# Six numbers of the mixers' scheduling tables in a hybrid attention and convolution layer: four priority offsets, two filler counts

## Chip, cores and metric

The kernel runs on one core of one Trainium2 chip. The metric is the device time of one execution in microseconds (us), given as the median of several runs.

## What is computed

One layer of a hybrid trunk, on x of 1 x 2048 x 1024 in float32. The mixers are sliding-window attention (8 query heads of 64, 2 key/value heads, blocks of 128, window 128, a learned sink per head) beside a gated short convolution of width 512. An MLP of 1024 to 4096 to 1024 with squared relu follows. Cut to what matters:

```
h = rms_norm(x, attn_norm_g)
z = h @ w_in                       # q, k, v, gate_b, gate_c, xc
q, k = rms_norm(q, q_norm_g), rms_norm(k, k_norm_g)
y_attn = swa_sink_attention(q, k, v, sinks)
y_conv = gate_b * short_conv(gate_c * xc, conv_w)
y = concatenate([rms_norm(y_attn, attn_out_g), rms_norm(y_conv, conv_out_g)])
x = x + y @ w_out
hm = rms_norm(x, mlp_norm_g)
x = x + square(relu(hm @ w_up)) @ w_down
```

## The kernel before

**Tiles and stages.** Each float32 operand of a large product is split in a high and a low part, and a product takes three matmul passes, lines 278, 279 and 280 of the helper `mm3`. The sequence is worked in four chunks of 512 positions, stages 0 to 3 here, of four blocks of 128 each; the blocks are b0 to b15, so stage 1 holds b4 to b7 and stage 3 holds b12 to b15. After the mixers the MLP follows: seven products in place of eight for each level of its blocks, up in line 1454 and down in line 1571, about 64% of the span.

**Attention of a block.** `qk_transpose` puts q and k on the partitions (matmuls ptq_b and ptk_b of L697 and L699, the splits into high and low parts of qt_b and kw on ScalarE and VectorE in L702 to L707). `softmax` makes the scores (matmuls psc_b, L724), copies and masks them (L732, L735), reduces the maximum (L737, L738), takes eight exponentials (L741) and the denominators (L745 to L748), and scales the probabilities (L749). `values` turns the probabilities (ptp_b, L760), splits them (ScalarE L766, VectorE L767; GpSimd masks them, L773, into pp_b), splits v into vz and vd (L787, L788), multiplies (po_b, L812: two matmuls with vz, then two with vd, for each of the two key/value heads), and moves the result out (L820, L821) and into the split operand at_b of the output projection (L824, L825). L826 to L828 and the tiny matmul pa_b (L833), copied in L835, give the attention norm.

**Work beside it.** TensorE is kept going by steps that have nothing to do with the block at hand: the generator `besides` yields after every three matmuls. In a stage they are the attention half of the output projection of the chunk before (pout, moved out by VectorE in L963), the convolution's products (pc_c, px_c, pb_c), the convolution half of this chunk's output projection (pout of yt_c, L963 too), the norm and transposition of the next chunk (L294, pt_a L306, L310, L311) and its projection pz. In stage 3, where there is no next chunk, the attention half of its own projection runs at its end, and `x_blocks` prepares operands of the MLP: it loads rows (L362), scales them (L368), transposes them on TensorE (pt_m, L374), puts them back with a gain on VectorE (L375), stores blocks to memory over the queue of SyncE (SP; xop, L345), and makes differences of blocks in place on VectorE (L388), which are stored too. An L388 that overwrites a block has to wait until the store that reads it has landed. SP also issues the weight loads (L247).

**What sets the order.** Two tables. `FILL[c]` says how many of those steps are pulled at which place of stage c: FILL[c][0] before and after the first scores, and FILL[c][t+1] at five places for block t, the fourth of them in `values` just ahead of the first po_b matmuls and the fifth between the two heads. `PRIO[stage][i]` is an offset with which the instructions of one part are put ahead of (positive) or behind (negative) others by the scheduler that writes each engine's order: 0 qk_transpose, 1 softmax, 2 the q and k norm of the next block, 3 the attention norm, 4 the first part of values, 5 the po_b matmuls, 6 the moving out of values, 7 the weights' splits, 8 the norm of `prepare`, 9 its transposition, 10 the convolution, 11 the moving out of the projection (L963), 12 and 13 the two parts of `x_blocks`. The fifth row of PRIO is that of what follows the mixers. Once written, the order of each engine is fixed, and each engine takes its instructions strictly in it.

**PSUM.** Three banks hold the products pout, pc_c, px_c, pb_c, pz ("mm"), four the attention, one the transpositions (pt_a, pt_m). A product that needs a bank waits until what stood there has been moved out, so L963 gives back an "mm" bank and L375 gives back the transposition bank.

Of the kernel before, what the change touches and what calls it, by code (L numbers as in the profile page):

```python
# [84 lines left out]


PRIO = (
# [5 lines left out]
)  # L93

FILL = (
# [4 lines left out]
)  # L100


# [1508 lines left out]
```

## Time and profile before

| | |
|---|---|
| median of 3 runs | 1916.22 us (1916.06 to 1918.76) |
| profiled execution | 1920.32 us |
| its span | 1918.6 us |
| TensorE (PE) busy | 1910.4 us, 8930 matmuls |
| VectorE (DVE), ScalarE (ACT), GpSimd (POOL) busy | 1202.4, 829.4, 276.2 us |
| start of the first ptq_b of b0, b4, b8, b12, and of the first MLP matmul | 45.3, 187.0, 357.3, 524.0, 695.2 us |

A row of the timeline gives the start in us, the duration in us, engine, line, operation, out<-in by name without numbers, sizes, how many neighbours are taken together, and in brackets the idle time of the engine before it with what ended it. A matmul's shown duration is modelled and longer than the distance to the next one; distances between starts tell what a matmul costs. A row of the table by stretches of time gives the stretch, its length, then for PE, PEld (weight load), DVE, ACT and POOL the busy us and in brackets the instructions, then the granted TensorE clock, the busy share of the DMA engines and GB/s.

### The profile page before, as it was taken

Reading aid. Unit: us, or ns where it says so; the run is one execution under the profiler, and the core shown is the slowest. Engines: PE = TensorE matmul, PEld = TensorE weight load, DVE = VectorE, ACT = ScalarE, POOL = GpSimd, SP = SyncE. Lnnn points to the kernel's source line nnn. Section 1 sums busy time; section 2 is a strip of 40 time slices with the busy share of each in tenths; the row PEclk is TensorE's granted clock in tenths of the full one; section 3 lists DMA queues with packets and bytes.
Section 4 is the critical chain, followed back from the end, with each engine's and each line's share of the span. In section 5 each row is a group of like instructions: output and inputs, shape, how many; then the busy total and the mean of one; then the engine's idle time right before and its main releaser. Section 6 shows DMA issues by size and latency. Waiting matters only on the chain.

```text
span 1918.6 us, 24557 instructions
## 1 busy us (share of the span) xinstructions
PE 1910.4 (100%) x8930; PEld 1592.5 (83%) x8930; DVE 1202.4 (63%) x1857; ACT 829.4 (43%) x1557; POOL 276.2 (14%) x477
## 2 busy tenths in 40 slices
PE   9999999999999999999999999999999999999999
PEld 8888888888888888888888888888888888888887
DVE  4895567448467759999778766766534334457531
ACT  5564345335444446444555545554322332232320
POOL 2123212312221112233101111111000000100000
PEclk9999999999999999999999999999999999999999
DMA  8984854564577688768566444438954456866631
GB/s 280 337 325 125 328 198 176 205 234 154 201 273 259 215 301 242 229 215 247 192 224 224 164 161 146 150 138 320 367 200 148 138 175 221 284 223 213 218 126 55
DMA packets 232792, 413.80 MB, mean 216 GB/s; under 512 B 51672, under 2 KB 136416, under 8 KB 219872
## 3 DMA queue, kind: packets, MB, share of 16 engines
q1 hardware_dynamic: 203696, 336.33, 51.8%
q0 software_dynamic: 15424, 51.40, 6.9%
q10 hardware_dynamic: 13552, 24.52, 3.4%
q8 instruction: 70, 1.15, 0.2%
q14 instruction: 50, 0.41, 0.1%
HBM read 286.35 MB, written 125.83 MB: 215 GB/s over the span
## 4 chain that ended last, share of the span: by engine, by line
PE 96%; DMA 2%; DVE 1%; ACT 1%; SPq 0%; POOL 0%; issue 0%; ACTq 0%; DVEq 0%
PE u L1454 32%; PE d L1571 32%; PE pout L278 3%; PE pout L280 3%; PE pout L279 3%; PE pz L278 2%; PE pz L280 2%; PE pz L279 2%; PE psc_b L724 1%; PE px_c L280 1%; PE px_c L278 1%; PE px_c L279 1%; PE pb_c L280 1%; PE po_b L812 1%; PE pb_c L279 1%; PE pb_c L278 1%
## 5 line engine op out<-in xcount | busy, mean ns | idle before, releaser
L1454 PE MATMUL u<-op_x,wop 128*128 128x512 f32 x2688 | 610.2, 389 | 0.0
L1571 PE MATMUL d<-op_w,op_f 128*128 128x512 f32 x2691 | 609.5, 389 | 0.0
L1454 PEld LDWEIGHTS u<-op_x,wop 128*128 128x128 f32 x2688 | 504.4, 188 | 105.6 <-DVE wop L453 0.4
L1571 PEld LDWEIGHTS d<-op_w,op_f 128*128 128x128 f32 x2691 | 505.0, 188 | 104.5
L434 DVE TENSOR_TENSOR op_f<-op_f 128x1024 fp32r<-128x1024 f32 x112 | 137.0, 1225 | 237.2 <-ACT op_f L433 237.2
L433 ACT CAST op_f<-op_f 128x1024 fp32r<-128x1024 f32 x112 | 117.7, 1051 | 353.1 <-DMA op_f<-fop 342.5
L452 ACT CAST wop<-wu 128x512 fp32r<-128x512 f32 x156 | 96.3, 620 | 92.4 <-PE u L1454 89.3
L453 DVE TENSOR_TENSOR wop<-wu,wop 128x512 fp32r<-128x512 f32 x156 | 111.2, 714 | 33.6 <-ACT wop L452 18.5
L1190 POOL DMA_DIRECT2D fop<-s x96 | 52.1, 542 | 441.8 <-DVE s L1193 437.3
L1196 DVE TENSOR_TENSOR u<-u,u 128x512 f32<-128x512 f32 x128 | 88.0, 687 | 19.0 <-PE u L1454 18.7
L434 DVE TENSOR_TENSOR op_w<-raw,op_w 128x1024 fp32r<-128x1024 f32 x56 | 68.4, 1223 | 25.4 <-ACT op_w L433 25.2
L433 ACT CAST op_w<-raw 128x1024 fp32r<-128x1024 f32 x56 | 58.8, 1051 | 45.0 <-PE d L1571 22.6
L1202 ACT ACTIVATE u<-u 128x512 f32<-128x512 f32 x64 | 40.5, 632 | 53.8 <-DVE u L1196 51.5
L741 ACT ACTIVATE sc_b<-sc_b,ngm_b 128x128 f32<-128x128 f32 x128 | 49.7, 390 | 29.4 <-DVE ngm_b L738 29.4
L773 POOL TENSOR_SCALAR_AFFINE_SELECT pp_b<-pp_b 128x512 fp32r<-128x512 f32 x60 | 41.2, 700 | 133.9 <-ACT pp_b L766 66.0
L1403 POOL DMA_DIRECT2D wds<-raw x16 | 8.5, 533 | 330.0 <-DVE raw L1401 330.0
L453 DVE TENSOR_TENSOR wop<-wu_s,wop 128x512 fp32r<-128x512 f32 x64 | 46.0, 720 | 11.4 <-ACT wop L452 11.2
L452 ACT CAST wop<-wu_s 128x512 fp32r<-128x512 f32 x64 | 39.4, 620 | 30.0 <-PE u L1454 26.8
L278 PE MATMUL pout<-w_wo,yt_c 128*128 128x512 f32 x128 | 51.5, 402 | 0.0
L280 PE MATMUL pout<-w_wo,yt_c 128*128 128x512 f32 x128 | 51.0, 398 | 0.0
L724 PE MATMUL psc_b<-kw,qt_b 128*128 128x256 f32 (+1 forms) x256 | 49.3, 285 | 1.1 <-DVE qt_b L703 0.8
L279 PE MATMUL pout<-w_wo,yt_c 128*128 128x512 f32 x128 | 50.3, 393 | 0.0
(265 smaller groups left out, 3106.4 us busy)
## 6 DMA issues: line engine op xcount, KB each, us to landing
op_f<-fop SPq DMA_DIRECT2D x112, 512.0 KB, 4.4
raw<-in_w_down_dram SPq DMA_DIRECT2D x72, 512.0 KB, 4.1
wu<-in_w_up_dram SPq DMA_DIRECT2D x128, 256.0 KB, 3.7
w_wo<-wo SPq DMA_DIRECT2D x24, 1024.0 KB, 6.8
fop<-s POOLq DMA_DIRECT2D x96, 256.0 KB, 2.6
fop<-u ACTq DMA_DIRECT2D x64, 256.0 KB, 2.6
op_x<-xop SPq DMA_DIRECT2D x28, 512.0 KB, 6.4
w_q<-q SPq DMA_DIRECT2D x12, 1024.0 KB, 6.7
```

Source lines behind the costliest of these rows:

```text
L278: nc.tensor.matmul(ps, st(0), mv(0), start=first, stop=False)
L279: nc.tensor.matmul(ps, st(0), mv(1), start=False, stop=False)
L280: last_sum[0] = nc.tensor.matmul(ps, st(1), mv(0), start=False, stop=last).ins
L433: nc.scalar.copy(op[:, 0], raw)
L434: nc.vector.tensor_tensor(op[:, 1], raw, op[:, 0].bitcast(F32), op=ALU.subtract)
L452: splits.append(nc.scalar.copy(hi, blk).ins)
L453: lows.append(nc.vector.tensor_tensor(lo, blk, hi.bitcast(F32), op=ALU.subtract).ins)
L724: nc.tensor.matmul(ps[:, j].rearrange("p s k -> p (s k)")[:, :nk], qt[:, pr, j, :], kw[:, r, kv, :, :].rearrange("p s k -> p (s k)")[:, :n ...
L1190: eng.dma_start(fop_dram[tb][ORDER_DOWN.index(i)][n // 2][:, n % 2], b)
L1196: return nc.vector.tensor_tensor(dst, ps, b, op=ALU.add).ins
L1454: nc.tensor.matmul(pt, wops[i][:, a, k, :], xops[tb, p][k // 2][:, b, k % 2, :], start=p not in GOES_ON and k + j == 0, stop=k + j == NB + ...
L1571: nc.tensor.matmul(ps[tb][j][:, cs], fs[tb][:, a, k, j * P : (j + 1) * P], w[:, b, k, cs], start=first and p not in GOES_ON and k + n == 0 ...
```

## The change

Four entries of PRIO and two of FILL get other numbers. No instruction is added or removed on any engine.

```diff
-    (60, 0, 160, -10, 30, 0, 20, -10, -20, 30, 0, 300, 0, 0),
-    (220, -60, -60, -50, 40, 0, 20, 40, -60, 280, 0, 0, 0, 0),
+    (60, 0, 160, -10, 30, 0, 20, -10, -20, 30, 0, 320, 0, 0),
+    (220, -60, -60, -50, 40, 0, -10, 40, -60, 280, 0, 0, 0, 0),
...
-    (200, 20, 180, 240, 0, 0, 40, 40, 240, 0, 0, 30, 0, 0),
-    (160, 80, 0, 10, 0, 0, 20, -20, -20, 0, 0, 120, 0, 0),
+    (200, 20, 0, 240, 0, 0, 40, 40, 240, 0, 0, 30, 0, 0),
+    (160, 80, 0, 10, 0, -10, 20, -20, -20, 0, 0, 120, 0, 0),
...
-    ((25, 15), (9, 16, 11, 8, 1), (9, 8, 13, 3, 2), (13, 12, 15, 6, 5), (9, 14, 11, 5, 3)),
+    ((25, 15), (9, 16, 11, 9, 1), (9, 8, 13, 3, 2), (13, 12, 15, 6, 5), (9, 14, 11, 5, 3)),
...
-    ((27, 6), (9, 9, 5, 6, 3), (6, 7, 7, 5, 5), (8, 13, 8, 7, 8), (11, 3, 10, 1, 2)),
+    ((27, 6), (9, 9, 5, 6, 3), (6, 7, 7, 5, 5), (8, 13, 8, 7, 8), (11, 3, 10, 4, 2)),
```

Each number made by itself in the kernel before, with the rest left as it was, moves the following. PRIO[0][11] (300 to 320) and PRIO[4][5] (0 to -10) move no row of any engine. PRIO[1][6] (20 to -10) and FILL[1][1][3] (8 to 9) move rows of stage 1. PRIO[3][2] (180 to 0) moves rows of stage 3 from b12 to b14. FILL[3][4][3] (1 to 4) moves rows at the end of stage 3, at b15. The rows of stage 0 and of the MLP stand in the same order on every engine, and so do those of stage 2 but for one L684 on VectorE at its start, which falls behind one L963.

The first place is TensorE at the end of stage 3, where block b15 multiplies its probabilities (po_b) beside the first half of the last output projection (pout). Before:

```order
L280 MATMUL pout_0_0_0_6647<-w_wo_0_6505,at_b_5845 128x512
L812 MATMUL po_b_0_6651<-pp_b_0_0_6602,vz 128x512
L278 MATMUL pout_0_0_0_6647<-w_wo_0_6505,at_b_5845 128x512
L279 MATMUL pout_0_0_0_6647<-w_wo_1_6506,at_b_5845 128x512
L812 MATMUL po_b_0_6651<-pp_b_0_0_6602,vz 128x512
L812 MATMUL po_b_0_6651<-pp_b_0_1_6603,vd 128x512 x2
L280 MATMUL pout_0_0_0_6647<-w_wo_0_6505,at_b_5845 128x512
```

The same place with the change:

```order
L280 MATMUL pout_0_0_0_6647<-w_wo_0_6505,at_b_5845 128x512
L812 MATMUL po_b_0_6661<-pp_b_0_0_6602,vz 128x512 x2
L812 MATMUL po_b_0_6661<-pp_b_0_1_6603,vd 128x512 x2
L278 MATMUL pout_0_0_1_6666<-w_wo_0_6505,at_b_6156 128x512
L279 MATMUL pout_0_0_1_6666<-w_wo_1_6506,at_b_6156 128x512
```

Before, the four po_b matmuls of the first head began after three of the twelve matmuls of the first pout; now they stand together behind all twelve. Those of the second head stand behind six matmuls of the next pout, and pa_b of b15 stands after six matmuls of the fourth pout instead of after nine of the third. On VectorE the L963 of the first pout goes ahead of b15's two L821.

The second place is VectorE in stage 3, where the softmax of b12 and the scores of b13 (sc_b_5452 and sc_b_5603) run beside the blocks of `x_blocks` (xt_m); rows with - are of before, those with + of the change:

```order
 L375 TENSOR_TENSOR xt_m_0_5440<-pt_m_0_1_5583,g_cols 128x512
 L747 TENSOR_TENSOR den_b_5488<-den_b_5488,es_b_5497 128x8
-L388 TENSOR_TENSOR xt_m_0_5440<-xt_m_0_5440 128x512
+L735 COPY_PREDICATED sc_b_5603<-later,psc_b_0_5604 128x128
 L748 RECIPROCAL den_b_5488<-den_b_5488 128x8
 L735 COPY_PREDICATED sc_b_5603<-later,psc_b_0_5604 128x128
 L749 TENSOR_TENSOR sc_b_5452<-sc_b_5452,den_b_5488 128x1024
-L735 COPY_PREDICATED sc_b_5603<-later,psc_b_0_5604 128x128
 L735 COPY_PREDICATED sc_b_5603<-later,psc_b_1_5612 128x128 x2
+L388 TENSOR_TENSOR xt_m_0_5440<-xt_m_0_5440 128x512
 L735 COPY_PREDICATED sc_b_5603<-later,psc_b_2_5620 128x128 x2
```

The first L388 of these blocks stands now behind the scaling of b12 (L749) and three more L735. On TensorE the transpositions of the two blocks just ahead of this place stand four matmuls earlier (pt_m of xt_m_0_5439, second half) and two matmuls earlier (pt_m of xt_m_0_5440, first half), and the four psc_b_3 of b12 stand together instead of one by one between pc_c matmuls; on SP one xop store goes ahead of one load of x, two ahead of another, and later one ahead of a weight load.

The third place is VectorE in stage 1, where L963 moves out the convolution half of chunk 1's output projection (pout_1_0_0 and on, one for each block of 128) while b5 is moved out (o_b, at_b) and b6 is in its softmax (den_b, sc_b). Before, beginning with the L963 of the first pout:

```order
L963 SCALAR_TENSOR_TENSOR x_1_0_3041<-pout_1_0_0_3073,rc_2148,x_1_0_3041 128x512
L827 TENSOR_TENSOR o_b_3100<-o_b_3100 128x256
L963 SCALAR_TENSOR_TENSOR x_1_1_3043<-pout_1_0_1_3131,rc_2148,x_1_1_3043 128x512
L311 TENSOR_TENSOR h_h_3050<-pt_a_1_4_3246,h_h_3049 128x4x128
L828 TENSOR_TENSOR o_b_3100<-o_b_3100 128x128
L747 TENSOR_TENSOR den_b_2891<-den_b_2891,es_b_2900 128x8
L963 SCALAR_TENSOR_TENSOR x_1_2_3045<-pout_1_0_2_3148,rc_2148,x_1_2_3045 128x512
L748 RECIPROCAL den_b_2891<-den_b_2891 128x8
L735 COPY_PREDICATED sc_b_3187<-later,psc_b_0_3188 128x128
L749 TENSOR_TENSOR sc_b_2855<-sc_b_2855,den_b_2891 128x1024
```

With the change:

```order
L747 TENSOR_TENSOR den_b_2894<-den_b_2894,es_b_2903 128x8
L821 TENSOR_TENSOR o_b_3104<-po_b_1_3099,o_b_3104 64x512
L748 RECIPROCAL den_b_2894<-den_b_2894 128x8
L963 SCALAR_TENSOR_TENSOR x_1_0_3010<-pout_1_0_0_3073,rc_2148,x_1_0_3010 128x512
L749 TENSOR_TENSOR sc_b_2858<-sc_b_2858,den_b_2894 128x1024
L311 TENSOR_TENSOR h_h_3019<-pt_a_1_4_3246,h_h_3018 128x4x128
L825 TENSOR_TENSOR at_b_3109<-o_b_3104,at_b_3109 128x512
L963 SCALAR_TENSOR_TENSOR x_1_1_3012<-pout_1_0_1_3095,rc_2148,x_1_1_3012 128x512
L963 SCALAR_TENSOR_TENSOR x_1_2_3014<-pout_1_0_2_3148,rc_2148,x_1_2_3014 128x512
```

The softmax of b6 (L747, L748, L749) has moved from behind the L963 of the second and third pout to ahead of them, and the L821 of b5's second head stands ahead of the first. On TensorE po_b of b5 and ptq_b of b7 come three matmuls later, and on ScalarE the eight exponentials of b6 go ahead of the L820 of b5's second head.

## Prediction

> **What bounds the kernel now.** I read the page's head first, then the table by stretches of time, then the waits of TensorE (PE).
>
> ```profile
> span 1918.6 us, 24557 instructions
> PE 1910.4 (100%) x8930; PEld 1592.5 (83%) x8930; DVE 1202.4 (63%) x1857; ACT 829.4 (43%) x1557; POOL 276.2 (14%) x477
> ```
>
> ```profile
> 200.00:400.00 200.00, 200.00 (x1015) 169.03 (x1014) 114.06 (x240) 84.36 (x234) 47.49 (x80) 1.00 0.61 233
> 400.00:600.00 200.00, 198.71 (x1029) 166.64 (x1028) 127.14 (x257) 93.25 (x245) 40.49 (x72) 1.00 0.56 208
> 600.00:700.00 100.00, 99.64 (x486) 82.72 (x485) 65.09 (x125) 35.11 (x90) 18.26 (x39) 1.00 0.70 239
> 700.00:800.00 100.00, 100.00 (x443) 82.84 (x442) 89.01 (x130) 61.52 (x101) 21.14 (x39) 1.00 0.85 263
> 582.00:585.00 3.00, 3.00 (x19) 2.56 (x17) 2.89 (x6) 0.43 (x1) 1.03 (x3) 1.00 0.43 107
> 555.00:582.00 27.00, 26.92 (x146) 22.64 (x145) 19.91 (x46) 18.15 (x57) 2.40 (x6) 1.00 0.90 319
> ```
>
> ```profile
> PE idle L579 <- POOL ident L172: 1.6, 1, 1.6
> PE psc_b L724 <- DVE qt_b L703: 0.8, 1, 0.8
> PE po_b L812 <- POOL pp_b L773: 0.4, 1, 0.4
> PE psc_b L724 <- DVE kw L706: 0.3, 1, 0.3
> ```
>
> ```profile
> 1911.80 2.91 PE L1571 MATMUL d<-op_w,op_f 128*128 128x512 f32 x15
> ```
>
> TensorE is the bound: of 1918.6 us it is idle in 1918.6 - 1910.4 = 8.2. Of these 1.6 are its wait for the identity matrix at the start, and 1918.6 - 1914.7 = 3.9 lie behind the last matmuls (1911.80 + 2.91), so that under 3 us of waits are left in the whole program. From 200 to 400 us, where stage 1 lies, it is idle for 0.00 us; from 400 to 600 for 1.29; in the first 100 us of MLP for none, the three other engines being busy less. An order that only moves work can win what TensorE waits, and little else: its matmuls are the same 8930. That caps a gain at a fifth of a per cent before anything else is known, and losses have no such cap.
>
> The Trainium skill, page "Perfetto Trace Analysis", section "Identifying the Most-Contended Engine", says that matmul busy time is no measure of TensorE's headroom and that the busy share of the weight loads is to be used. Taken so, 83% would leave 17% of the span, some 326 us, to win, and the cap above would be wrong. The rows speak against it here: from 700 to 800 us TensorE has no gap, and its weight loads are busy for 82.84 of 100 us.
>
> The profiled execution took 1920.32 us, 4.1 above the median of 1916.22. The terms below are differences of start times within that one execution, and I put them on the median.
>
> **Term 1, FILL[3][4][3] from 1 to 4 (end of stage 3, b15).** A matmul of 512 columns is followed by the next one after 0.23 us; what a row stands later than that is loss.
>
> ```profile
> 672.27 0.40 PE L812 MATMUL po_b<-pp_b,vd 128*128 128x512 f32 x1
> 673.03 0.50 PE L812 MATMUL po_b<-pp_b,vd 128*128 128x512 f32 x1 [0.36 <-POOL pp_b L773]
> 673.37 0.40 PE L280 MATMUL pout<-w_wo,at_b 128*128 128x512 f32 x1
> 673.60 0.39 PE L278 MATMUL pout<-w_wo,at_b 128*128 128x512 f32 x1
> ...
> 681.55 0.40 PE L278 MATMUL pout<-w_wo,at_b 128*128 128x512 f32 x1
> ```
>
> ```profile
> 671.95 2.31 POOL L773 TENSOR_SCALAR_AFFINE_SELECT pp_b<-pp_b 128x512 fp32r<-128x512 f32 x3 [0.21 <-DVE pp_b L767]
> ```
>
> ```profile
> 677.40 0.68 DVE L825 TENSOR_TENSOR at_b<-o_b,at_b 128x512 fp32r<-128x512 f32 x1
> ```
>
> The second vd matmul of the first head starts 673.03 - 672.27 = 0.76 after the first, 0.53 too late, and the next one 0.34 after it, 0.11 too late: 0.64 us. It waits for GpSimd's second masking: three take 2.31 us from 671.95, about 0.77 each, so that the first of them is done at about 672.7 and the last at 674.3. In the new order nine more pout matmuls stand ahead of the first po_b, and its second vd starts at about 674.0, the second head's at about 676.1. Both are behind what they need, by 1.3 and 1.8 us, and the wait goes: **-0.64 us**. What is late next? The second head's results come 1.4 us later (676.35 in place of 674.96 for its last matmul), and so does the split L825, which ended at 677.40 + 0.68 = 678.08; counting that the second pout's L963 now goes ahead of it, it ends at about 679.7. The first matmul that reads it stood at 681.55 and will stand at about 680.8. That leaves 1.1 us, and pa_b, which went six matmuls further back, about 0.4. Bounds: -0.64 and 0, the latter if one of these margins is used up.
>
> **Term 2, PRIO[3][2] from 180 to 0, at the transpositions.**
>
> ```profile
> 563.00 0.39 PE L278 MATMUL pc_c<-h_h,w_wc 128*128 128x512 f32 x1
> 563.47 0.66 PE L374 MATMUL pt_m<-ident,xt_m 128*128 128x128 f32 x4
> ```
>
> ```profile
> 562.52 0.30 DVE L735 COPY_PREDICATED sc_b<-later,psc_b 128x128 f32<-128x128 int32 x1
> 562.73 0.68 DVE L375 TENSOR_TENSOR xt_m<-pt_m,g_cols 128x512 f32<-128x512 f32 x1
> 563.33 1.21 DVE L737 TENSOR_REDUCE ngm_b<-sc_b 128x8 f32<-128x1024 f32 x1
> 564.46 0.68 DVE L375 TENSOR_TENSOR xt_m<-pt_m,g_cols 128x512 f32<-128x512 f32 x1
> ```
>
> The transposition of 563.47 waits for the bank that L375 gives back at 563.41 and starts 0.24 late. Four matmuls earlier it would be due at about 562.5, before that L375 is through. But b12's last scores, which VectorE's queue needs ahead of it, also come together and up to 0.8 us earlier, so that the wait stays about as long. The transposition behind it then wants the bank at about 563.9, and its L375 is queued behind the reduction L737 of 1.21 us. It could cost 0.24 + 0.1 more, or the earlier scores could clear the way. Value **0**, bounds -0.3 (the late start goes) and +0.4.
>
> **Term 3, the same number, at the stores.** The longest wait of the mixers' later part hangs on a store.
>
> ```profile
> 593.63 0.39 PE L278 MATMUL pb_c<-h_h,w_wb 128*128 128x512 f32 x1
> 594.31 0.39 PE L724 MATMUL psc_b<-kw,qt_b 128*128 128x256 f32 x1 [0.28 <-DVE kw L706]
> ...
> 594.91 0.40 PE L280 MATMUL pb_c<-h_h,w_wb 128*128 128x512 f32 x1
> 596.07 0.50 PE L724 MATMUL psc_b<-kw,qt_b 128*128 128x256 f32 x2 [0.77 <-DVE qt_b L703]
> ```
>
> ```profile
> 591.91 0.69 DVE L388 TENSOR_TENSOR xt_m<-xt_m,xt_m 128x512 f32<-128x512 f32 x1 [2.23 <-DMA xop<-xt_m]
> ```
>
> ```profile
> 570.13 0.63 SPq L247 DMA_DIRECT2D w_wc<-wc  x1
> ...
> 582.93 0.32 SPq L247 DMA_DIRECT2D w_wx<-wx  x1
> 583.44 2.31 SPq L345 DMA_DIRECT2D xop<-xt_m  x2
> ```
>
> ```profile
> w_wx<-wx SPq DMA_DIRECT2D x1, 1024.0 KB, 7.8
> xop<-xt_m SPq DMA_DIRECT2D x1, 256.0 KB, 8.0
> ```
>
> Here TensorE loses 0.45 + 0.93 = 1.4 us. The chain back: scores of b14 need qt_b and kw from VectorE, VectorE stood still for 2.23 us at an L388, and that waits for the store issued at 583.44, which needed 8.0 us because the 1 MB load issued half a us ahead of it shares the engines. Between VectorE's L388 and those scores the change moves nothing. But earlier, the second place in the order rows, the first L388 stands behind an L749 and three L735, some 1.9 us later: L749 takes 1.22 (its row stands in term 4) and an L735 0.2 (562.52 to 562.73). Its store is issued later, and SP, which works in order, issues the 1 MB load w_wc of 570.13 later too. From 555 to 582 us the DMA engines are 0.90 busy, so a delay can be carried on; from 582 to 585, just ahead of the store in question, they are 0.43 busy, so it has room to end. I take the latter, the nearer row: **0**. Bounds: +1.9 if the whole delay arrives, and -1.4 if the shift by chance brings the store home before VectorE comes to it.
>
> **Term 4, FILL[1][1][3] from 8 to 9 and PRIO[1][6] from 20 to -10 (stage 1).** TensorE has no idle time there, so there is nothing to win beyond 0.1 us of late starts.
>
> ```profile
> 303.71 0.74 DVE L963 SCALAR_TENSOR_TENSOR x<-pout,rc,x 128x512 f32<-128x512 f32 x1
> ...
> 307.15 1.22 DVE L749 TENSOR_TENSOR sc_b<-sc_b,den_b 128x1024 f32<-128x1024 f32 x1
> ```
>
> The L963 give back the product banks, and the softmax rows L747, L748 and above all L749 with its 1.22 us now stand between the first two of them, with b5's L825 besides. Three banks and groups of twelve matmuls at 0.23 give a bank about 5.4 us until it is wanted again, and the queue is some 2.6 us longer ahead of the second L963: it should mostly fit, with little left for the fourth pout. Value **+0.2**, bounds -0.1 and +1.2 (one L749 in full).
>
> **PRIO[0][11] and PRIO[4][5]** move no row on any engine: 0.
>
> **Sum.** -0.64 + 0 + 0 + 0.2 = -0.44 us: 1916.22 - 0.44 = **1915.8 us**, and the profiled execution of 1920.32 by the same sum 1919.9. A difference of 0.2% here is 3.8 us, about what a measurement of this kernel can tell from no change; the forecast is no change.
>
> **The rivals.**
>
> *The store comes later (ends slower).* Term 3 takes its upper end: the delay of up to 1.9 us goes from L388 through the stores and the w_wc load to the store at 583.44, VectorE stands still that much longer, and TensorE waits for qt_b. 1916.22 - 0.64 + 1.9 = 1917.5. For it: 0.90 busy DMA and strict order on SP. Against it: the 0.43 just ahead. It decides the sign as soon as that store lands over 0.64 us later than before.
>
> *The stage 1 banks run out (slower).* Term 4 takes 1.2: 1916.22 - 0.64 + 1.2 = 1916.8. For it: the L749 between two L963. Against it: the 5.4 us and a stage without a gap.
>
> *It doesn't do what it says.* Two of the six numbers are dead, and the wait of term 1 may only move to the next reader (at_b or pa_b of b15): 1916.2.
>
> *The store's wait goes by chance (faster).* 1916.22 - 0.64 - 1.4 = 1914.2, or -0.11%.
>
> *TensorE falls back to a slow phase.* At the start it runs at half rate:
>
> ```profile
> 6.64 2.08 PE L555 MATMUL pz<-w_q,h_a 128*128 128x512 f32 x4 [0.45 <-ACT w_q L593]
> ...
> 11.88 2.31 PE L555 MATMUL pz<-w_q,h_a 128*128 128x512 f32 x9
> ```
>
> Four matmuls in 2.08 us, then nine in 2.31, 0.52 against 0.26 each, and the change comes some 8 us after the first matmul at 1.58. If a wait in stage 3 grew so long that this came back, it would cost the growth, about 2.6 us from 0.77, and half of some 8 us: 1916.22 - 0.64 + 2.6 + 4 = 1922.2. Against it: the longest gap is 0.77 us, and the granted clock is 1.00 in every stretch shown (it is given as 1.00 in the slow start too, so the row can't exclude a short phase). The Trainium skill, page "TensorE: Matmul & The Clock Gate", section "🔬 Part 1: The HAM clock gate (the "warmup" mystery)", puts the clock at half after an idle window of about 3.4 us and needs as much steady work to lift it; the start agrees in its factor of two, and no row in the middle of this run shows a fall.
>
> **How the numbers follow.** Forecast 0.50, with its own range of 1915.1 to 1916.4; the later store 0.18; banks 0.12; nothing done 0.08; the store's wait gone 0.07; slow phase 0.05. Faster by over 0.2% needs below 1912.4, that is all the waits named here and another 1.5 us: 0.02, out of the store's wait gone. Slower by over 0.2%, above 1920.1, is the slow phase: 0.05. Within: 0.93. The range goes from 1913.9, the store's wait gone and term 2's 0.3 with it, to 1918.7, where the later store and the banks come together (1916.22 - 0.64 + 1.9 + 1.2).
>
> **What would show it.** Term 1: the wait of po_b for GpSimd's pp_b is gone from TensorE's waits, and none for at_b or o_b has come. Term 2: the starts around pt_m at 562 to 564 us. Term 3: how long that store takes and whether VectorE's 2.23 us before L388 is longer or shorter; psc_b's waits of 0.8 and 0.3 follow it. Term 4: still 200.00 busy from 200 to 400 us. A change of over 2 us either way would make the prediction wrong in its reasons, since no wait but that of the store has so much to give.

## The result, and the profile after

The changed kernel takes **1921.09 us** (median of 12 runs, 1918.0 to 1923.92) against **1916.25 us** for the kernel before in the same comparison (12 runs, 1915.45 to 1920.28). The ratio is 1.0017, with a 95% interval of 1.0009 to 1.0025: slower by about 3 us. The ratio is not the quotient of the two medians, which lie 4.84 us apart; its interval reaches from 1.7 to 4.8 us. The forecast was 1915.8 and the range ended at 1918.7, so the measured time lies above it.

The profiled execution took 1923.0 us. The head of its page, and its table by stretches of time with the columns as before (PE busy, then PEld, DVE, ACT, POOL, the granted clock, the DMA share, GB/s):

```profile
span 1921.3 us, 24566 instructions
PE 1909.6 (99%) x8930; PEld 1590.3 (83%) x8930; DVE 1203.0 (63%) x1857; ACT 828.1 (43%) x1557; POOL 277.5 (14%) x477
```

```profile
200.00:400.00 200.00, 199.41 (x1010) 168.22 (x1009) 113.85 (x239) 83.91 (x234) 48.38 (x80) 1.00 0.61 231
400.00:600.00 200.00, 198.22 (x1026) 166.31 (x1025) 125.55 (x254) 92.46 (x244) 40.20 (x71) 1.00 0.58 211
```

The work is the same. TensorE is idle for 11.7 us of the span, it was 8.2, and stage 1, which had no gap, has 0.6. Its waits:

```profile
PE pz L555 <- ACT w_q L593: 1.6, 1, 1.6
...
PE ptq_b L697 <- ACT sc_b L732: 1.0, 1, 1.0
PE psc_b L724 <- DVE qt_b L703: 0.8, 1, 0.8
PE pa_b L833 <- DVE o_b L828: 0.8, 2, 0.6
PE psc_b L724 <- DVE kw L706: 0.6, 1, 0.6
PE u L1454 <- DVE wop L453: 0.4, 1, 0.4
PE pt_m L374 <- DVE xt_m L375: 0.4, 1, 0.4
PE u L1454 <- ACT wop L452: 0.3, 1, 0.3
PE u L1454 <- ACT u L1209: 0.2, 1, 0.2
```

The wait of po_b for GpSimd is gone. New are pa_b behind VectorE's L828, pt_m behind L375, and three waits of the MLP's u, which stands in the part of the program whose order didn't change. Term 1's place on TensorE:

```profile
674.66 0.61 PE L812 MATMUL po_b<-pp_b,vz 128*128 128x512 f32 x2
675.11 0.62 PE L812 MATMUL po_b<-pp_b,vd 128*128 128x512 f32 x2
675.56 0.39 PE L278 MATMUL pout<-w_wo,at_b 128*128 128x512 f32 x1
```

The two vd matmuls take 675.56 - 675.11 = 0.45 us together, the full rate. Terms 2 and 3, TensorE and then VectorE:

```profile
562.84 0.39 PE L280 MATMUL pc_c<-h_h,w_wc 128*128 128x512 f32 x1
563.61 0.66 PE L374 MATMUL pt_m<-ident,xt_m 128*128 128x128 f32 x4 [0.39 <-DVE xt_m L375]
```

```profile
562.87 0.68 DVE L375 TENSOR_TENSOR xt_m<-pt_m,g_cols 128x512 f32<-128x512 f32 x1
```

```profile
593.27 0.69 DVE L388 TENSOR_TENSOR xt_m<-xt_m,xt_m 128x512 f32<-128x512 f32 x1 [2.57 <-DMA xop<-xt_m]
```

The transposition is 563.61 - 562.84 - 0.23 = 0.54 us late, it was 0.24: it comes earlier in the order, the L375 that gives its bank back doesn't (562.87 + 0.68 = 563.55). VectorE stands still for 2.57 us ahead of L388, it was 2.23. And the MLP on TensorE near 995 us:

```profile
993.62 1.52 PE L1454 MATMUL u<-op_x,wop 128*128 128x512 f32 x6
995.49 0.73 PE L1454 MATMUL u<-op_x,wop 128*128 128x512 f32 x2 [0.34 <-ACT wop L452]
996.65 4.66 PE L1454 MATMUL u<-op_x,wop 128*128 128x512 f32 x18 [0.43 <-DVE wop L453]
```

Below, "late" means: the distance between the starts of two neighbouring matmuls, less the median distance of such a pair of shapes in the same trace, added up over a place. Each kernel has one trace for each time that it is listed below.

### The profile page after: what moved, and what is told of

Read it like the earlier page. It is cut to its first block, busy times and chain, and to the rows that moved or that the text cites. A ratio compares the mean times of both kernels' runs of the same rounds, so it can differ in the third digit from the quotient of the medians.

```text
span 1921.3 us, 24566 instructions
## 1 busy us (share of the span) xinstructions
PE 1909.6 (99%) x8930; PEld 1590.3 (83%) x8930; DVE 1203.0 (63%) x1857; ACT 828.1 (43%) x1557; POOL 277.5 (14%) x477
## 5 line engine op out<-in xcount | busy, mean ns | idle before, releaser
L434 DVE TENSOR_TENSOR op_f<-op_f 128x1024 fp32r<-128x1024 f32 x112 | 136.9, 1224 | 234.2 <-ACT op_f L433 234.0
L433 ACT CAST op_f<-op_f 128x1024 fp32r<-128x1024 f32 x112 | 117.6, 1051 | 352.9 <-DMA op_f<-fop 338.0
L434 DVE TENSOR_TENSOR op_w<-raw,op_w 128x1024 fp32r<-128x1024 f32 x56 | 68.4, 1222 | 27.4 <-ACT op_w L433 27.4
L433 ACT CAST op_w<-raw 128x1024 fp32r<-128x1024 f32 x56 | 58.8, 1051 | 46.0 <-PE d L1571 24.2
L278 PE MATMUL pout<-w_wo,at_b 128*128 128x512 f32 x124 | 48.9, 394 | 0.0
```

Source lines behind the costliest of these rows:

```text
L278: nc.tensor.matmul(ps, st(0), mv(0), start=first, stop=False)
L433: nc.scalar.copy(op[:, 0], raw)
L434: nc.vector.tensor_tensor(op[:, 1], raw, op[:, 0].bitcast(F32), op=ALU.subtract)
```

## The experiments

**First, the change in pieces**, each beside the kernel before on the same chip. The two numbers that move no row:

```diff
-    (60, 0, 160, -10, 30, 0, 20, -10, -20, 30, 0, 300, 0, 0),
+    (60, 0, 160, -10, 30, 0, 20, -10, -20, 30, 0, 320, 0, 0),
...
-    (160, 80, 0, 10, 0, 0, 20, -20, -20, 0, 0, 120, 0, 0),
+    (160, 80, 0, 10, 0, -10, 20, -20, -20, 0, 0, 120, 0, 0),
```

> Only the two numbers that move no row, PRIO[0][11] and PRIO[4][5]. Every theory expects the time of the kernel before, within 0.05%, and the same waits in the mixers (0.64 us late starts at po_b of b15, 1.4 at the scores of b14). The theory that the rise is scatter from run to run also expects some of its runs 2 to 4 us above the others, as in the kernel before. If this kernel is slower by over 1 us, something other than the order of the engines is changed.

Measured: 1918.00 us against 1917.92 for the kernel before, ratio 1.0005 (0.9997 to 1.0014), runs from 1915.85 to 1921.99. It is the same program, and its runs, like those of the kernel before here (35 runs, 1915.23 to 1923.03), spread over 6 us and more. So the comparison resolves about 0.1%, and one trace is one draw out of such a spread: this one has a span of 1914.1 us, 4.5 below that of the first trace of the same program.

```profile
PE idle L579 <- POOL ident L172: 1.6, 1, 1.6
PE po_b L812 <- POOL pp_b L773: 0.4, 1, 0.4
```

These two are all its waits of TensorE. The waits of b14, which the prediction priced at 1.4 us, are not in it; the one of po_b is. The ground is the store ahead of b14's scores: it took 8.0 us in the first trace and 6.1 in this one, and VectorE's wait for it at L388 was 2.23 and 0.35.

The two numbers of stage 1:

```diff
-    (220, -60, -60, -50, 40, 0, 20, 40, -60, 280, 0, 0, 0, 0),
+    (220, -60, -60, -50, 40, 0, -10, 40, -60, 280, 0, 0, 0, 0),
...
-    ((25, 15), (9, 16, 11, 8, 1), (9, 8, 13, 3, 2), (13, 12, 15, 6, 5), (9, 14, 11, 5, 3)),
+    ((25, 15), (9, 16, 11, 9, 1), (9, 8, 13, 3, 2), (13, 12, 15, 6, 5), (9, 14, 11, 5, 3)),
```

> Only FILL[1][1][3] 8 to 9 and PRIO[1][6] 20 to -10 (stage 1). If the loss is made of the waits that the trace of the changed kernel shows near the rows moved, this kernel carries about +1.0 us: a wait of pa_b of b7 for VectorE's L828 at about 368 us (0.75) and a late product bank at about 305 (0.25). If the loss comes from the loads of the MLP, which the stores of stage 3 push back, it carries no more than that, +1.0 or less, and the MLP shows no wait of TensorE at u14 near 995 us. If stage 1 alone makes the whole loss, +3 us or more.

Measured: 1918.42 against 1917.92, ratio 1.0008 (0.9999 to 1.0018). pa_b of b7 is 0.8 us late, the MLP not at all. The size fits the waits near the rows that moved; the interval just includes no change.

The priority of the q and k norm in stage 3:

```diff
-    (200, 20, 180, 240, 0, 0, 40, 40, 240, 0, 0, 30, 0, 0),
+    (200, 20, 0, 240, 0, 0, 40, 40, 240, 0, 0, 30, 0, 0),
```

> Only PRIO[3][2] 180 to 0 (stage 3, the one number that changes the order on SP's queue). Local waits: +0.6 us (0.3 more at the transposition pt_m near 563 us, 0.3 more at the scores of b14). If the loss comes from the MLP's loads, this kernel has the larger part of it: +2 us or more, with waits of TensorE at u14 near 995 us behind the splits L452 and L453. If stage 1 makes the loss, within 0.6 us of the kernel before.

Measured: 1918.37 against 1917.92, ratio 1.0005 (0.9997 to 1.0014). pt_m is 0.6 us late (0.36 before), b14 1.3, the MLP near 995 us 0.8. The 2 us or more that the theory of late loads expected aren't here.

The filler number of b15:

```diff
-    ((27, 6), (9, 9, 5, 6, 3), (6, 7, 7, 5, 5), (8, 13, 8, 7, 8), (11, 3, 10, 1, 2)),
+    ((27, 6), (9, 9, 5, 6, 3), (6, 7, 7, 5, 5), (8, 13, 8, 7, 8), (11, 3, 10, 4, 2)),
```

> Only FILL[3][4][3] 1 to 4 (b15). By the prediction's term 1: -0.6 us, the wait of po_b for GpSimd gone and no new one in its place. If the loss comes from a shift of the MLP against its loads whatever shifts it, this kernel is slower too, by 1 us or more, though its only local effect is a gain.

Measured: 1917.85 against 1917.92, ratio 0.9999 (0.9990 to 1.0009). The 0.68 us at po_b of b15 are gone and no wait of at_b or pa_b of b15 has come; 1.0 us stands late in the MLP.

**Second, the places.** The changed kernel once more, no edit:

> The changed kernel once more, unaltered, beside the kernel before on the same chip: slower by 0.1 to 0.25% (2 to 5 us). By the theory of fixed waits its trace has again 0.75 us late at pa_b of b7, 0.5 at pt_m near 563 us, and a wait at the scores of b14 of over 0.6 us; by the theory that the MLP's loads come late whatever runs, the late starts at u14 near 995 us (1.5 us) come again. By the theory of scatter they don't, and the starts at b14 differ by over 0.5 us from the first trace.

Measured: 1919.14 against 1918.25, ratio 1.0009 (1.0000 to 1.0018). Late: 0.83 at pa_b of b7, 0.83 at pt_m, 1.0 at b14, 2.1 in the MLP. The fixed waits are there, the MLP's too; b14's differs from the first trace by 1.5.

Stage 1's number of filler steps alone (the FILL lines of stage 1 as above, PRIO as before):

> Only FILL[1][1][3] 8 to 9. Theory of the missing step: pa_b of b7 is 0.7 us late here with this number alone (PRIO[1][6] has no part in it), and the product bank at about 305 us is not late. Rival (PRIO[1][6] moves VectorE's work): pa_b of b7 is under 0.2 us late.

Measured: a single run of 1918.18 us, without an interval; pa_b of b7 is 0.82 us late in its trace. TensorE's po_b of b7 and its pa_b, and then GpSimd and VectorE of the same trace:

```profile
352.29 0.63 PE L812 MATMUL po_b<-pp_b,vz 128*128 128x512 f32 x2
...
365.21 0.35 PE L833 MATMUL pa_b<-mean,o_b 128*128 128x1 f32 x2 [0.59 <-DVE o_b L828]
```

```profile
353.06 1.22 POOL L773 TENSOR_SCALAR_AFFINE_SELECT pp_b<-pp_b 128x512 fp32r<-128x512 f32 x2 [1.70 <-PE po_b L812]
354.36 0.27 POOL L192 TENSOR_SCALAR ssq_b<-ssq_b 128x10 f32<-128x10 f32 x1
354.71 2.00 POOL L193 TENSOR_TENSOR rq_b<-ssq_b,mhalf 128x10 f32<-128x10 f32 x1
```

```profile
356.74 0.82 DVE L684 TENSOR_TENSOR z<-z,rq_b 128x640 f32<-128x640 f32 x1 [2.03 <-POOL rq_b L193]
...
364.78 0.28 DVE L828 TENSOR_TENSOR o_b<-o_b 128x128 f32<-128x128 f32 x1
```

Read from above: the first po_b of b7 lets GpSimd mask (1.22 us), behind which stands the power for rq_b (2.00 us); VectorE waits for that at L684 and from there on works without a pause until L828, which pa_b reads. From po_b to pa_b that is 365.21 - 352.29 = 12.92 us. In the kernel with the dead numbers, whose order is that of before, it is the same distance, and TensorE has just so much to do in it:

```profile
351.95 0.63 PE L812 MATMUL po_b<-pp_b,vz 128*128 128x512 f32 x2
...
364.87 0.35 PE L833 MATMUL pa_b<-mean,o_b 128*128 128x1 f32 x2
```

No wait, and no slack. A step pulled early is missing later: with the ninth step ahead of b4's po_b, one step less lies between b7's first po_b and its pa_b. There a step is six matmuls of pz with 256 columns at 0.12 us, 0.7 us together, and 73 matmuls stand in place of 79. To put it back, I tried two places. After the first head's po_b:

```diff
-    ((25, 15), (9, 16, 11, 9, 1), (9, 8, 13, 3, 2), (13, 12, 15, 6, 5), (9, 14, 11, 5, 3)),
+    ((25, 15), (9, 16, 11, 9, 1), (9, 8, 13, 3, 2), (13, 12, 15, 6, 5), (9, 14, 11, 5, 2)),
```

> The changed kernel with FILL[1][4][4] 3 to 2, so that the last po_b of b7 stand one step (0.7 us) earlier and the cover between them and pa_b of b7 is as long as before the change. Theory that the ninth filler step pulled early is missing at the end of the stage: the wait of pa_b of b7 for L828 goes (0.75 us late to under 0.1), and nothing else in stage 1 moves; -0.7 us against the changed kernel. Rival, that L828 is late because VectorE's order in stage 1 moved: the wait stays at 0.6 or grows.

Measured: 1921.03 against 1918.25, ratio 1.0013 (1.0004 to 1.0022). pa_b of b7 is still 0.83 us late, the expectation was wrong: this moves the second head's po_b alone, and the chain begins at the first. Ahead of both:

```diff
-    ((25, 15), (9, 16, 11, 9, 1), (9, 8, 13, 3, 2), (13, 12, 15, 6, 5), (9, 14, 11, 5, 3)),
+    ((25, 15), (9, 16, 11, 9, 1), (9, 8, 13, 3, 2), (13, 12, 15, 6, 5), (9, 14, 11, 4, 3)),
```

> The changed kernel with FILL[1][4][3] 5 to 4, so that both heads' po_b of b7 stand one step (0.7 us) earlier and the distance from the first of them to pa_b of b7 is as long as before the change. Theory of the GpSimd chain: po_b of the first head releases GpSimd's two maskings, behind which stands the 2 us power for rq_b, on which VectorE stands still and after which it works without a pause up to L828; the longer distance takes the late start at pa_b from 0.75 to under 0.1 us, so -0.7 us in the stage. Rival (VectorE's order alone makes L828 late): it stays over 0.5.

Measured: 1919.16 against 1917.64, ratio 1.0007 (0.9999 to 1.0016). TensorE in its trace:

```profile
351.91 0.63 PE L812 MATMUL po_b<-pp_b,vz 128*128 128x512 f32 x2
...
364.84 0.35 PE L833 MATMUL pa_b<-mean,o_b 128*128 128x1 f32 x2
```

12.93 us again, with 79 matmuls, all of it work, and the wait is gone: the chain is shown. In the time, this kernel lies 2.1 us below the changed one on the same chip (1921.26 in the third set of runs below), more than the 0.7 us; the two intervals overlap, so the difference is not resolved.

For the stores, the changed kernel with them on GpSimd's queue:

```diff
-            nc.sync.dma_start(
+            nc.gpsimd.dma_start(
                 dst.rearrange("p (h t c) -> p h t c", h=2, t=NB)[:, :, t], b.rearrange("p (h c) -> p h c", h=2)
             )
```

> The changed kernel with the xop stores of x_blocks issued by GpSimd instead of SP, so that they stand in another queue than the 1 MB weight loads. Theory that the scores of b14 wait for a store held up behind a load in SP's queue: the store lands within 4 us, VectorE no longer stands still ahead of L388, and the waits of psc_b of b14 (0.8 and 0.6 us in the changed kernel) go: -1.5 us or so against the changed kernel. Rival, that all transfers share the same engines and a store is slow whichever queue it is in: it still lands after 7 us or more and the waits stay within 0.5 us. A third outcome: GpSimd's issuing delays its maskings L773 and po_b waits appear.

Measured: 1931.63 against 1918.25, ratio 1.0071 (1.0059 to 1.0084). The waits at b14 go, but VectorE and GpSimd now hold each other up: an L388 waits 5.4 us for a store, and TensorE 7.9 for an L375 behind it. In this trace po_b also waits 3.3 us for GpSimd's maskings, as in the third outcome; that GpSimd's issuing is the cause of it isn't shown. It is no clean test of the queue, since two of its first stores still took over 8 us, and the median of all is 3.2. TensorE in its trace:

```profile
591.80 1.12 PE L374 MATMUL pt_m<-ident,xt_m 128*128 128x128 f32 x4 [7.92 <-DVE xt_m L375]
...
593.57 0.63 PE L280 MATMUL pb_c<-h_h,w_wb 128*128 128x512 f32 x1
594.00 0.63 PE L278 MATMUL pb_c<-h_h,w_wb 128*128 128x512 f32 x1
...
596.23 0.40 PE L279 MATMUL pb_c<-h_h,w_wb 128*128 128x512 f32 x1
596.47 0.39 PE L280 MATMUL pb_c<-h_h,w_wb 128*128 128x512 f32 x1
```

After a gap of 7.92 us matmuls stand 0.43 us apart instead of 0.23, until about 595.8. The granted clock of a short stretch shows it (the third number from the end):

```profile
589.50:595.50 6.00, 3.70 (x12) 3.02 (x13) 5.09 (x8) 0.81 (x2) 2.94 (x5) 0.50 0.62 261
```

By rows of half a us the clock falls at about 589.0, 5.1 us after TensorE fell idle (591.80 - 7.92 = 583.88), and is back at about 595.8, 4.0 us after the first matmul behind the gap.

**Third, the MLP.** The changed kernel with PRIO[3][2] back at 180:

> The changed kernel with PRIO[3][2] back at 180. If that number carries the loss in the store chain and in the MLP: faster than the changed kernel by about 2 us (0.3 at pt_m, 0.6 at b14, over 1 in the MLP near 995 us), so within 0.05% of the kernel before (0.9 of stage 1 against 0.64 of b15). If the loss in the MLP comes with the other numbers or with chance, the late starts near 995 us come here too and the time stays at that of the changed kernel.

Measured: 1918.43 against 1917.64, ratio 1.0005 (0.9997 to 1.0014). The MLP is 2.5 us late near 995 us without that number, so that number isn't the cause by itself.

The changed kernel without the two numbers of stage 1:

> The changed kernel without the two numbers of stage 1, so PRIO[3][2] and FILL[3][4][3] alone. Theory of fixed waits: 0.9 us faster than the changed kernel, no wait at pa_b of b7. If PRIO[3][2] brings the waits of the MLP, the late starts near 995 us are over 1 us here; if chance brings them, they can be anything from 0 to 2.5.

Measured: 1918.31 against 1917.64, ratio 1.0004 (0.9995 to 1.0013); MLP 1.2 us late, pa_b of b7 in time.

The changed kernel a third time:

> The changed kernel a third time. Fixed waits again: 0.75 us late at pa_b of b7, 0.5 to 0.8 at pt_m of 562 us, none at po_b of b15. Theory that the changed order also brings late loads in the MLP: over 1.5 us of late starts between 980 and 1020 us for the third time of three; theory of chance: under 1 us, as in the kernels with part of the change.

Measured: 1921.26 against 1917.64, ratio 1.0018 (1.0010 to 1.0027); MLP 1.9 us late, the third time of three. Up to here no kernel with FILL[3][4][3] at 1 had more than 0.8 us in the MLP, and every one with 4 and the stores on SP had about 1.0 or more. That made a theory: what TensorE gains at b15 it gives back there. The changed kernel with that number back at 1:

> The changed kernel with FILL[3][4][3] back at 1 (so PRIO[3][2] and stage 1 remain). Theory that the gain at b15 is given back in the MLP: late starts between 980 and 1020 us fall under 0.8 us (they were 1.9 to 2.4 in three executions of the changed kernel), the 0.64 at po_b of b15 comes back, and the time falls by about 1 us or more against the changed kernel. Theory of chance: the late starts there are as likely 2 us as 0, and the kernel is 0.6 us slower than the changed one.

Measured: 1920.31 against 1917.11, ratio 1.0014 (1.0005 to 1.0023); MLP 1.1 us late, po_b of b15 0.69. The theory expected under 0.8 and a faster kernel: it falls in this form. The number alone a second time:

> FILL[3][4][3] 1 to 4 alone, a second time. Theory of the gain given back: no wait of po_b of b15, and again about 1 us or more of late starts between 980 and 1020 us, so within 0.05% of the kernel before. Theory of chance: those late starts differ from the first time's 1.0 by more than 0.8 either way or are absent.

Measured: 1917.18 against 1917.11, ratio 1.0001 (0.9992 to 1.0010); MLP 0.7 late. With 2 in place of 4:

```diff
-    ((27, 6), (9, 9, 5, 6, 3), (6, 7, 7, 5, 5), (8, 13, 8, 7, 8), (11, 3, 10, 1, 2)),
+    ((27, 6), (9, 9, 5, 6, 3), (6, 7, 7, 5, 5), (8, 13, 8, 7, 8), (11, 3, 10, 2, 2)),
```

> The kernel before with FILL[3][4][3] at 2, three matmuls more ahead of po_b of b15 instead of nine. GpSimd's masking is done at 672.98 by the first trace and the second vd would start at about 673.2: the 0.64 us go as with 4. Theory of the gain given back: late starts of 1 us or more between 980 and 1020 us too; if it is the order with 4 in particular that disturbs the MLP's loads, under 0.8 and 0.5 us faster than the kernel before.

Measured: 1917.53 against 1917.11, ratio 1.0003 (0.9994 to 1.0012). 0.45 us remain at po_b of b15, more than expected: the three matmuls went ahead, but the two that had stood between the po_b went too. MLP 0.9 late. And the kernel before:

> The kernel before, unaltered, once more with its trace. Fixed waits: 0.64 us late at po_b of b15, 0.3 at pt_m near 562 us, under 0.15 at pa_b of b7. What differed between its first trace and that of the kernel with the two dead numbers is scatter and can be anything here: the start (2.2 to 4.9 us late), ptq_b of b1 (0 to 1.4), the scores of b14 (0.4 to 2.8). Between 980 and 1020 us under 0.8 by the theory that late loads there come with FILL[3][4][3].

Measured: a single run of 1917.63 us; MLP not late, b14 0.4, po_b of b15 0.7, the start 4.4. The traces with the stores on SP together (us late; "start" is from about 4 to 40 us, "stage 1" its two numbers or the filler number alone; the kernel with the dead numbers is the second of "before"):

| kernel | start | ptq_b of b1 | pa_b of b7 | pt_m | b14 | po_b of b15 | MLP, 980 to 1020 |
|---|---|---|---|---|---|---|---|
| before, three traces | 4.2, 2.8, 4.4 | 0.9, 0.0, 0.0 | 0.1 | 0.36 | 2.1, 0.4, 0.4 | 0.7 | 0.6, 0, 0 |
| stage 1, two traces | 2.6, 2.2 | 0.0 | 0.8 | 0.3 | 0.4, 2.2 | 0.7 | 0, 0 |
| PRIO[3][2] | 2.2 | 0.1 | 0.1 | 0.6 | 1.3 | 0.7 | 0.8 |
| PRIO[3][2], stage 1 | 4.6 | 0.0 | 0.8 | 0.6 | 0.5 | 0.7 | 1.1 |
| FILL[3][4][3] at 4 (two), at 2 | 4.9, 2.5, 2.2 | 0.1, 0.9, 1.0 | 0.1 | 0.3 | 0.8, 0.5, 0.4 | 0, 0, 0.45 | 1.0, 0.7, 0.9 |
| both of stage 3 | 2.6 | 0.8 | 0.1 | 0.6 | 0.4 | 0 | 1.2 |
| FILL[3][4][3], stage 1 | 2.3 | 0.0 | 0.8 | 0.3 | 0.4 | 0 | 2.5 |
| changed kernel, three traces | 3.4, 2.2, 2.7 | 1.3, 0.2, 1.4 | 0.8 | 0.6, 0.8, 0.6 | 2.4, 1.0, 0.4 | 0 | 2.4, 2.1, 1.9 |
| changed, with the first, the second cover | 2.3, 2.3 | 0.4, 0.0 | 0.8, 0.1 | 0.6 | 2.8, 0.4 | 0 | 2.6, 1.5 |

The last column as rows of the table by stretches: the kernel before (first trace, then the later one), the changed one, and the changed one with PRIO[3][2] taken back. The number in brackets behind TensorE's time counts its matmuls.

```profile
980.00:1020.00 40.00, 39.99 (x176) 32.42 (x175) 36.73 (x55) 30.47 (x49) 6.47 (x12) 1.00 0.71 252
```

```profile
980.00:1020.00 40.00, 40.00 (x178) 33.05 (x177) 38.83 (x56) 31.32 (x52) 7.02 (x13) 1.00 0.73 258
```

```profile
980.00:1020.00 40.00, 39.01 (x167) 30.71 (x166) 36.64 (x55) 28.01 (x45) 6.47 (x12) 1.00 0.72 257
```

```profile
980.00:1020.00 40.00, 38.94 (x167) 30.63 (x166) 38.03 (x55) 31.18 (x51) 6.47 (x12) 1.00 0.69 252
```

11 matmuls fewer than 178, at 0.23 each, are the 2.5 us. What makes TensorE late is loads. ScalarE copies each op_x load (L433) before VectorE splits it (L434). The third of the op_x loads issued after 940 us, in the changed kernel and in that with the dead numbers:

```profile
967.24 1.05 ACT L433 CAST op_x<-op_x 128x1024 fp32r<-128x1024 f32 x1 [5.13 <-DMA op_x<-xop]
```

```profile
958.51 1.05 ACT L433 CAST op_x<-op_x 128x1024 fp32r<-128x1024 f32 x1 [1.38 <-DMA op_x<-xop]
```

The MLP's first matmul starts at 695.76 in the one and 691.39 in the other. Counted from it, the copy starts after 271.5 and 267.1 us, and TensorE's first late matmul in the changed kernel (995.49) comes only after 299.7: the load is late first. The waits of 45 us, beginning 263.6 us after that first matmul (959.4 to 1004.4 and 955 to 1000), in the same two kernels:

```profile
ACT op_x L433 <- DMA op_x<-xop: 14.8, 3, 5.1
DVE op_x L434 <- ACT op_x L433: 10.4, 4, 5.1
```

```profile
ACT op_x L433 <- DMA op_x<-xop: 8.3, 4, 3.8
DVE op_x L434 <- ACT op_x L433: 4.2, 5, 2.1
```

ScalarE waits 14.8 us for op_x in the one and 8.3 in the other, and VectorE behind it 10.4 and 4.2. In the 40 us up to 984.4 and 980 VectorE is busy for 25.7 us and 28.5, so that it comes to the tight stretch with more left to do. Measured in the same place of the program, all 18 traces follow this wait of ScalarE: the six with 8.3 to 12.6 us (the three of the kernel before, the two of stage 1, and the changed kernel with the stores on GpSimd) have 0 to 0.6 us late, the five with 12.7 to 13.1 have 0.7 to 1.2, the seven with 13.7 to 15.2 have 1.1 to 2.6. So there is a point, at about 12.6 us, up to which the waits are covered. That VectorE can't make them up because it is nearly full (36.6 to 38.8 of the 40 us in the rows above) is argued, not tested.

**What is shown and what stays open.** The 5 traces without a number of stage 3 have on average 0.1 us late in this stretch, none over 0.6; the 12 with one (stores on SP) have 1.6, none under 0.7. So the association is with either number of stage 3, not with one of them. The changed kernel with the stores on GpSimd has both and nothing late there, but it comes to the MLP 12 us later, so it decides little. How loads 300 us after stage 3 come to land later, though every row of the MLP stands in the same order, is open. The order of SP's queue can't be all of it, since FILL[3][4][3] alone leaves it as before: the op_x loads are issued at the same distances from TensorE's matmuls in all of these traces until about 946 us, and from there they drift apart. That chance has a part in it can't be excluded: the times of the pieces don't resolve 0.1%. None of the kernels tried is faster than the kernel before by more than its interval, so there was no better version to run.

## Why the prediction was wrong

Two steps failed. The prediction put the MLP at nothing because none of its rows moves, and there the changed kernel's three traces are 1.9 to 2.4 us late. And in stage 1 it looked for a cost only at the rows that moved, and missed 0.7 us at pa_b of b7, where a step is missing. By its own sign of being wrong, a change of over 2 us, it was wrong in its reasons.

- **Term 1 (-0.64) was right, in mechanism and size.** In all traces with 4 the late 0.7 us is gone, in all with 1 it is there, and at_b and pa_b of b15 are in time.
- **Term 2 (0, bounds -0.3 and +0.4)** is +0.3. The step "the wait stays about as long" failed: VectorE's L375 ended no earlier, so the earlier transposition waits 0.54 in place of 0.24. The second one, which I feared, is not late (0.08).
- **Term 3 (0, bounds -1.4 and +1.9)** had the right chain but priced one draw. The store that took 8.0 us in the first trace took 6.1 and 6.2 in the other two of the same order, with the same load ahead of it, so that load alone doesn't make the 8.0. The wait at b14 makes 0.4 to 2.2 late in nine traces with PRIO[3][2] at 180 (0.8 on average) and 0.4 to 2.8 in eight with 0 and the stores on SP (1.2). Its part in the loss is not resolved.
- **Term 4 (+0.2, bounds -0.1 and +1.2)** is +0.9, in size near its upper end. The bank that I named makes 0.2 of it; the other 0.7 are pa_b of b7, 63 us further on, where the filler step is missing. That the sum lies inside the bounds is luck: the upper one stood for an L749 in front of a bank. The step that failed is to read a stage without idle time as one with "nothing to win" and to look for a cost only at the rows that moved; without idle time there is no slack either.
- **The sum** of the mixers is then about +0.5 (-0.69 + 0.3 + 0.9), not -0.44: the sign was wrong by that alone. Another 1.9 us (2.1 against 0.2 on average) lie in the MLP, to which the prediction gave nothing since no row of it moved. Together that is 2.4 us, inside the measured 1.7 to 4.8. I took the MLP for a part without waits, from a table in steps of 100 us: there VectorE is busy for 89.01 from 700 to 800 and for only 78.15 and 79.58 in the two steps around 1000 us, which hide the tight stretch from 980 to 1020. None of the named rivals has this: the later store (1917.5) and the banks (1916.8) are slower for other reasons.
- **The base.** The first trace was 4.1 us above its median, and the prediction noted that and went on. The other traces of the same program show what that was: the waits at b14, at ptq_b of b1 and at the start are drawn anew in each execution.
- **The slow phase** did not come in the changed kernel. Its estimate of 4 us was too high: the gap of 7.92 us in the kernel with the stores on GpSimd cost 8.1 of waiting and about 1.7 in slow matmuls behind. The Trainium skill, page "TensorE: Matmul & The Clock Gate", section "🔬 Part 1: The HAM clock gate (the "warmup" mystery)", gives about 3.4 us of work until the full clock is back; the trace comes near it, with 4.0 us from 591.8 to 595.8. The prediction feared that the row of the clock can't show a short phase; in the middle of the run it does, with 0.50.

## What to carry to other kernels

A kernel whose bound engine is nearly full has slack of a few tenths of a us at many places: a filler step pulled early must be followed to the end of its pool and set against the chain that it covered, counted from where that chain begins (the first po_b, not the last). An order that doesn't change isn't a time that doesn't change: look for the stretch in which a second engine is nearly as full as the first one, in steps short enough to show it (40 us here, where 100 hid it), and for the loads that it waits for. And before a wait is priced from a trace, see in a second trace of the same program whether it is there.

## What the runs showed of the hardware

One program's runs spread from 1915.2 to 1923.0 us on one chip at a granted clock of 0.999 or 1.00. Transfers land at other times in each execution: in three traces of one order the 256 KB store ahead of b14's scores took 8.0, 6.1 and 6.2 us, and the start was 4.2, 2.8 and 4.4 us late. After a gap of 7.92 us TensorE ran at about half rate for 4.0 us (0.43 us a matmul); the granted clock of that whole execution is given as 0.998 and the waits show nothing of it, but the stretch from 589.5 to 595.5 has 0.50. GpSimd's power on 128x10 took 2.00 us, longer than a masking of 128x512 (0.61).
